# Second MLP of a decoder trunk: 11 of 16 pairs of up blocks by a 2x2 block scheme over tokens

## The chip, the cores and the metric

The program runs on one core of one Trainium2 chip. The metric is device time in microseconds (us), the median of three runs. The profile is one further execution of the same program, taken by the hardware profiler; its span runs from its first to its last instruction.

## The reference

Only the part that the change touches is given in full. The trunk has two layers; each has a mixer (multi-scale pooling in the first, stick-breaking attention in the second) and a squared-ReLU MLP, and each of the four is set between RMS norms.

```python
D_MODEL, SEQ, DEPTH = 1024, 512, 2
D_FF = 4 * D_MODEL
...
def sq_relu_mlp(h, w_up, w_down):
    u = jnp.matmul(h, w_up)
    return jnp.matmul(jnp.square(jax.nn.relu(u)), w_down)
...
        h = rms_norm(x, mlp_pre_g[layer])
        x = x + rms_norm(sq_relu_mlp(h, w_up[layer], w_down[layer]), mlp_post_g[layer])
```

All values are float32, h has 512 rows (tokens) of 1024, w_up is 1024 x 4096 and w_down 4096 x 1024.

## The kernel before

**Two parts for every operand.** A float32 operand is split into a high part (rounded to the matmul's format) and a low part, the rest. A product takes three matmuls: high by high, high by low, low by high. A split is a copy to the high part on ACT and a subtraction on DVE (`split`, L411 to L413; for weights `weight`, L140 to L155, whose lines L152 and L154 are the two steps and L142 the load).

**Up blocks.** The hidden dimension of 4096 is cut into 32 blocks of 128, numbered j. The loop `up_block` (L835) computes one block transposed: 128 hidden units by 512 tokens in one PSUM bank, over 8 slices of 128 of the contraction, three matmuls each, so 24 matmuls of 512 columns (lines L840, L841 and L842). Their moving operand are the normalised inputs `xnh` and `xnl`, which are high and low parts of [128, 8, 512]. `up` (L750) then has ACT do ReLU out of PSUM (L759) and the square (L760).

**Down products.** `Seven` (L630) computes the down projection for a group of blocks by a 2x2 block scheme with seven products in place of eight (halves of the tokens, of the group's blocks and of the output columns). The groups hold 2, 3, 3, 3 and 3 pairs of blocks (`GROUPS`, L25), so 28 of the 32 blocks; the last four go through `contract` (L554) with plain products. A product i of a group needs a combination of squares, `left(i)` (L669, L678; on POOL in the second MLP), and a combination of down weights, `right(i)` (L690, L697; on DVE), each split into parts by `split`. `make(i)` calls both, two products ahead, with two buffers each. Its matmuls are on L724: 18 of 512 columns for a group of three pairs, 12 for the first group. Each result is added to `y` by DVE out of PSUM (L736), or copied the first time (L731, L733).

**Order.** `mlp(l, mp, update)` (L738) is called for both layers. For each group g it loops over the seven products; behind each of the first six it issues one `up` block of the next group (in group 0 one more ahead of the loop), and the operands of the product after the next. In the last group those are the four blocks for `contract`. The order in which an engine gets its instructions in this part is not written by hand: a planner lays them out by their readiness and by the order in which the program issues them. Matrices stream from HBM by SP's queue; up weights go through two buffers `raw` into three buffers of parts (`w`) and a fourth (`wx`). PSUM has 8 banks of 512 columns; a group's products hold up to four at once, an up block one. The tiles `xt` hold the residual stream, `y` are four tiles of their own. The work behind the last down products is `Update` (L465): norm, gain, residual sum, store.

In the second MLP the first four blocks (j 0 to 3) are done in halves of 256 tokens ahead of group 0, while the last tokens of the input are still being normalised. Then group 0 runs beside the blocks 4 to 9, groups 1 to 3 beside six blocks each, and group 4 beside the last four.

## Time and profile before

| what | value |
|---|---|
| median of three runs | 887.29 us (887.13 to 887.39) |
| the profiled execution, its own time | 887.58 us |
| its span | 885.8 us |
| second MLP's first four up blocks | 561.0 to 584.9 us |
| its groups 0 to 4 | 584.9 to 861.5 us |
| `contract`, norm, residual sum and stores | 861.5 to 885.8 us |
| granted TensorE clock, mean | 0.998 |

The engines are PE (matmul), PEld (its weight loads, which lie beside the matmuls), DVE, ACT, POOL and SP. A row of the grouped view gives line, engine, operation, output<-input, shapes and count, then busy time in all and mean ns of one, then idle time ahead of them and what ended it. A row of the view by windows gives for a stretch of time its length, and busy time and instruction count of each engine. In the timeline a row is the start in us, the duration, and the instruction; the end of a matmul is modelled, so the step from one start to the next is its price.

### The profile page before, as it was taken

The page shows a single profiled execution, that of the slowest core. Times are in us where ns is not written, and L with a number is a line of the kernel's source. Part 1 is how long each engine was busy: PE and PEld are TensorE (multiplying, and loading weights), DVE is VectorE, ACT ScalarE, POOL GpSimd, SP SyncE. Part 2 cuts the span into 40 slices and gives each one's busy share as a digit, 9 for nine tenths or more (in the row PEclk, how much of TensorE's full clock was granted, in tenths as well). Part 3 has the DMA queues.
Part 4 walks back from the last instruction along what each step waited for, and adds up shares of the span by engine and source line. Part 5 has one row for each costly group of instructions (what it writes and reads, how often), then busy time and mean ns, then how long its engine had stood idle before and what let it go on. Part 6 is the DMA issues. An engine that isn't in the chain of part 4 may idle for free.

```text
span 885.8 us, 11988 instructions
## 1 busy us (share of the span) xinstructions
PE 875.6 (99%) x4628; PEld 765.3 (86%) x4628; DVE 693.7 (78%) x711; ACT 526.9 (59%) x878; POOL 85.2 (10%) x83
## 2 busy tenths in 40 slices
PE   9999999999999999999999999999999999999996
PEld 7998888888888888888888888998888888888885
DVE  5965898988979967656999985774897867977866
ACT  6758657667888736355888454465554454544631
POOL 2200000000000005000000001020310401303103
PEclk9999999999999999999999999999999999999999
DMA  7453557369697730875645655634324053142202
GB/s 287 162 203 124 187 203 274 132 215 344 249 344 260 274 130 1 321 296 204 212 152 165 209 184 166 231 134 146 116 98 163 24 176 110 48 154 84 64 8 95
DMA packets 47391, 153.86 MB, mean 174 GB/s; under 512 B 4656, under 2 KB 8714, under 8 KB 47334
## 3 DMA queue, kind: packets, MB, share of 16 engines
q1 hardware_dynamic: 47186, 153.09, 48.7%
q8 instruction: 36, 0.59, 0.3%
q14 instruction: 21, 0.17, 0.1%
q10 hardware_dynamic: 148, 0.02, 0.0%
HBM read 122.54 MB, written 30.54 MB: 173 GB/s over the span
## 4 chain that ended last, share of the span: by engine, by line
PE 93%; DVE 3%; DMA 2%; ACT 1%; issue 1%; POOL 0%; POOLq 0%; DVEq 0%; SPq 0%; ACTq 0%
PE ps L724 28%; PE ps L840 15%; PE ps L841 15%; PE ps L842 15%; PE ps L1124 3%; PE ps L453 2%; PE ps L455 2%; PE ps L454 2%; PE ps L1285 2%; PE ps L1200 2%; PE ps L979 2%; PE ps L955 1%; PE ps L1276 1%; DMA w<-kept 1%; ACT xn L416 1%
## 5 line engine op out<-in xcount | busy, mean ns | idle before, releaser
L724 PE MATMUL ps<-w,a 128*128 128x512 f32 x1176 | 265.3, 379 | 0.3
L840 PE MATMUL ps<-xnh,w 128*128 128x512 f32 (+1 forms) x704 | 253.6, 362 | 0.0
L841 PE MATMUL ps<-xnl,w 128*128 128x512 f32 (+1 forms) x704 | 253.3, 360 | 0.1
L842 PE MATMUL ps<-xnh,w 128*128 128x512 f32 (+1 forms) x704 | 253.2, 360 | 0.0
L724 PEld LDWEIGHTS ps<-w,a 128*128 128x128 f32 x1176 | 222.1, 189 | 32.5 <-ACT a L412 1.1
L842 PEld LDWEIGHTS ps<-xnh,w 128*128 128x128 f32 x704 | 133.4, 190 | 15.6
L841 PEld LDWEIGHTS ps<-xnl,w 128*128 128x128 f32 x704 | 133.4, 190 | 15.5 <-DVE xnl L413 0.3
L840 PEld LDWEIGHTS ps<-xnh,w 128*128 128x128 f32 x704 | 132.8, 190 | 16.2 <-ACT xnh L412 0.4
L152 ACT CAST w<-raw 128x1024 fp32r<-128x1024 f32 x56 | 58.6, 1046 | 85.4 <-PE ps L842 84.7
L736 DVE TENSOR_TENSOR y<-ps,y 128x512 f32<-128x512 f32 x124 | 83.9, 687 | 31.6 <-PE ps L724 31.4
L154 DVE TENSOR_TENSOR w<-raw,w 128x1024 fp32r<-128x1024 f32 x56 | 69.2, 1238 | 46.3 <-ACT w L152 46.3
L412 ACT CAST w<-e 128x1536 fp32r<-128x1536 f32 (+1 forms) x30 | 41.7, 1391 | 43.6 <-DVE e L697 33.7
L413 DVE TENSOR_TENSOR a<-r,a 128x768 fp32r<-128x768 f32 (+1 forms) x60 | 60.8, 1014 | 0.9 <-ACT a L412 0.9
L413 DVE TENSOR_TENSOR w<-e,w 128x1536 fp32r<-128x1536 f32 (+1 forms) x30 | 50.9, 1698 | 9.8 <-ACT w L412 9.6
L412 ACT CAST a<-r 128x768 fp32r<-128x768 f32 (+1 forms) x60 | 47.1, 785 | 16.7 <-POOL r L678 10.5
L1223 DVE TENSOR_TENSOR_SCAN e<-u,begin 128x1280 f32<-128x1280 f32 x16 | 44.9, 2808 | 13.4 <-ACT u L1214 13.3
L483 POOL TENSOR_TENSOR y<-y,grow 128x512 f32<-128x512 f32 x8 | 12.1, 1510 | 340.7 <-ACT xn L416 340.6
L413 DVE TENSOR_TENSOR w<-w,w 128x1536 fp32r<-128x1536 f32 (+1 forms) x20 | 34.6, 1729 | 11.2 <-ACT w L412 11.0
L412 ACT CAST w<-xn 128x1536 fp32r<-128x1536 f32 (+1 forms) x20 | 27.9, 1394 | 25.4 <-PE ps L724 25.4
L412 ACT CAST w<-w 128x1536 fp32r<-128x1536 f32 (+1 forms) x20 | 27.9, 1394 | 20.8 <-PE ps L724 18.9
L413 DVE TENSOR_TENSOR w<-xn,w 128x1536 fp32r<-128x1536 f32 (+1 forms) x20 | 33.0, 1650 | 8.0 <-ACT w L412 7.9
L759 ACT ACTIVATE r<-ps 128x512 f32<-128x512 f32 x56 | 33.1, 591 | 7.4 <-PE ps L842 7.4
(190 smaller groups left out, 1228.3 us busy)
## 6 DMA issues: line engine op xcount, KB each, us to landing
raw<-in_wup SPq DMA_DIRECT2D x64, 512.0 KB, 3.3
w<-kept SPq DMA_DIRECT2D x42, 512.0 KB, 5.9
w<-in_wdn SPq DMA_DIRECT2D x8, 1536.0 KB, 6.1
xn<-in_wdn SPq DMA_DIRECT2D x16, 768.0 KB, 4.9
kept<-wx SPq DMA_DIRECT2D x20, 512.0 KB, 3.0
kept<-apart SPq DMA_DIRECT2D x16, 512.0 KB, 3.4
through<-turn SPq DMA_DIRECT2D x7, 896.0 KB, 3.5
moved<-through SPq DMA_DIRECT2D x28, 224.0 KB, 3.8
```

What stands on the lines that cost most here:

```text
L152: nc.scalar.copy(hi, raw)
L154: nc.vector.tensor_tensor(out=lo, in0=raw, in1=hi.bitcast(F32), op=ALU.subtract)
L412: latest["act"] = nc.scalar.copy(hi, src)
L413: latest["dve"] = nc.vector.tensor_tensor(out=lo, in0=src, in1=hi.bitcast(F32), op=ALU.subtract)
L724: nc.tensor.matmul(bank, a[:, x, q, TS[t]], by_twos(w[:, z, q], NS[0]), start=start and q == 0 and k == 0, stop=q == self.n - 1 and k == 2 ...
L736: nc.vector.tensor_tensor(out=part, in0=bank, in1=part, op=ALU.add)
L759: nc.scalar.activation(split_up(r, 256), in_order(pu, 256), ACT.Relu)
L840: nc.tensor.matmul(pu[:, cols], wh[:, k, :], xh, start=k == 0, stop=False)
L841: nc.tensor.matmul(pu[:, cols], wh[:, k, :], xl, start=False, stop=False)
L842: nc.tensor.matmul(pu[:, cols], wl[:, k, :], xh, start=False, stop=k == KC - 1)
L1124: nc.tensor.matmul(bank, a[x][q], in_turn(w[q // 2][z][:, cols], 512), start=(i == 0 or not linked) and q == 0 and n == 0, stop=q == 3 and ...
L1223: nc.vector.tensor_tensor_scan(out=e[:, ::-1], data0=us[a][:, 1:][:, ::-1], data1=begin[:, ::-1], initial=0.0, op0=ALU.mult, op1=ALU.max,)
```

## The change

**Pairs.** Of the second MLP's up blocks, j 0 to 9 stay as they are (`PAIRED = 10`). The blocks 10 to 31 are taken as 11 pairs, q 0 to 10. A pair is a product of 2x2 blocks: two blocks of hidden units, two halves of the contraction, two halves of the tokens (256 each). It is done with seven products (`Pair.PRODUCTS`): each product is 4 slices x 3 matmuls of 256 columns, so a pair takes 84 matmuls of 256 columns where it took 48 of 512.

**Sums of the inputs.** Four combinations of quarters of the inputs, t1 to t4, are made once, during group 0, by `Sums`: ten additions and subtractions of 1024 columns on DVE, then four splits (ACT and DVE). Their parts lie in the buffer `wx`, in the tiles that `y` had, and t4 in a quarter of `xnh` and `xnl` themselves.

**Sums of the weights.** For each pair, S1 to S4 are made from the two raw weight blocks by four DVE operations of 512 columns (S3 in place of a21). Five splits follow: A (the whole first block, 1024 columns), B (S3 and a22, 1024 columns), S1, S2 and S4 (512 columns each). For S2 the low part is a subtraction on DVE, as before. For the other four (`BY_DMA`) ACT makes the high part and then writes its negative into the low part's place, and a DMA issued from POOL adds the raw values to it there.

**Results.** The seven products are added up partly in PSUM: those of a pair lie in two halves of one bank, and product 2 in a second bank. Each product is followed by one read of 256 columns: copies by ACT behind 1, 6 and 7, additions by DVE behind 2, 4 and 5, the ReLU by ACT behind 3. ReLU and square follow when a quarter or a half of the result is whole.

**Order.** `FIVE` writes where the products go: in groups 1 to 3 three pairs (a, b, c) of the next group are spread over seven cells, one behind each product of `Seven`; group 4 has two pairs, for the last four blocks. The operands of the next pair are prepared behind products of the one before; those of q 0 during group 0. A pair's raw weights use both `raw` buffers, and are loaded behind product 5 of the pair two before.

**The residual.** In the second MLP `y` now lies in the tiles of `xt`; `xt` is stored to HBM ahead of group 0 and loaded again near the end of group 4, into the tiles that `y` had.

```diff
+PAIRED = 10
+BY_DMA = "A B S1 S4".split()
...
-        for j in range(NJ):
+        for j in range(PAIRED if l else NJ):
             want(("up", l, j), wup[l, j])
...
+    class Sums:
...
+            self.homes = {1: (own[1], rest[1]), 2: rest[2:], 3: (own[0], rest[0]), 4: (high["12"], low["12"])}
...
+            self.steps = [
+                [(3, "h22", "h12", minus), (3, 3, "l22", plus), (3, 3, "l12", minus)],
+                [3, (1, "h12", "h11", minus)],
+                [(1, 1, "l12", plus), (1, 1, "l11", minus)],
+                [(2, "h22", 1, minus), (2, 2, "l22", plus), 1],
+                [(4, "h21", 2, minus), (4, 4, "l21", plus), 2],
+                [4],
+                [],
+            ]
...
+    class Pair:
...
+        PRODUCTS = {
+            1: ("a11", "b11", 0), 2: ("a12", "b21", 2), 3: ("s4", "b22", 0), 4: ("a22", "t4", 1),
+            5: ("s1", "t1", 0), 6: ("s2", "t2", 0), 7: ("s3", "t3", 1),
+        }
...
+        def load(self):
+            self.raw = [wts.tile([P, D], F32, tag="raw", bufs=2, name=name("raw")) for _ in range(2)]
+            for n, raw in enumerate(self.raw):
+                nc.sync.dma_start(raw, wup[self.l, self.j + n])
+
+        def split(self, what, src, hi, lo):
+            nc.scalar.copy(hi, src)
+            if what in BY_DMA:
+                nc.scalar.mul(lo, hi.bitcast(F32), -1.0)
+                nc.gpsimd.dma_start(lo, src, accum_op=ALU.add)
+            else:
+                nc.vector.tensor_tensor(out=lo, in0=src, in1=hi.bitcast(F32), op=ALU.subtract)
...
+        def prepare(self, behind):
+            on = nc.vector.tensor_tensor
+            if behind == 0:
+                self.load()
+                return
+            (a11, a12), (a21, a22) = ([x[:, c] for c in NS] for x in self.raw)
+            if behind == 1:
+                self.block(0)
+                both = spare_tile()
+                self.s1, self.s2 = both[:, NS[0]], both[:, NS[1]]
+                on(out=self.s1, in0=a21, in1=a22, op=ALU.add)
+                on(out=a21, in0=a11, in1=a21, op=ALU.subtract)
+            elif behind == 2:
+                self.block(1)
+                on(out=self.s2, in0=self.s1, in1=a11, op=ALU.subtract)
+            elif behind == 6:
+                self.third("S2", self.s2)
+            elif behind == 5:
+                self.third("S1", self.s1)
+                self.s4 = work.tile([P, D], F32, tag="grow", name=name("s4"))[:, NS[0]]
+                on(out=self.s4, in0=a12, in1=self.s2, op=ALU.subtract)
+            elif behind == 3:
+                self.third("S4", self.s4)
...
+        def product(self, i):
+            left, right, at = self.PRODUCTS[i]
+            if at == 2:
+                self.other = ps()
+            bank = self.other[:, :256] if at == 2 else self.bank[:, 256 * at : 256 * at + 256]
...
+            for k in range(4):
+                ws, xs = TS[k], [in_turn(x[:, k], 256) for x in (xh, xl)]
+                nc.tensor.matmul(bank, wh[:, ws], xs[0], start=start and k == 0, stop=False, skip_group_check=True)
+                nc.tensor.matmul(bank, wh[:, ws], xs[1], start=False, stop=False, skip_group_check=True)
+                nc.tensor.matmul(bank, wl[:, ws], xs[0], start=False, stop=k == 3, skip_group_check=True)
...
+            if i in (1, 6, 7):
+                nc.scalar.copy(out, src)
+            elif i in (2, 4, 5):
+                nc.vector.tensor_tensor(out=out, in0=src, in1=out, op=ALU.add)
...
+    FIVE = (
+        "a1 a2 a7 a6,a4 a5 b1 b2,a3 b7 b6,b4 b5 c1,c2 b3 c7,c6 c4 c5,c3",
+        "a1 a2 a7,a6 a4 a5,a3 b1 b2,b7 b6 b4 b5,b3,,",
+    )
     def mlp(l, mp, update):
...
-        y = y_tiles()
+        y = y_tiles() if l == 0 else [x[:, :D] for x in xt]
...
+            saved = dram.tile([T, P, D], F32, tag="saved", name="saved")
+            for t in range(T):
+                nc.sync.dma_start(saved[t], xt[t][:, :D])
+            sums = Sums()
+            pairs = [Pair(j, l, mp, sums) for j in range(PAIRED, NJ, 2)]
...
+            plan.update({(0, n): [(-1, int(x)) for x in w] for n, w in enumerate(("", "", "", "0", "12", "65", "3"))})
...
+        def ready(g, i):
+            if g == 0:
+                sums.step()
+            for q, which in plan[g, i]:
+                if q >= 0:
+                    multiply(g, q, which)
+                if which != 7 and which != 4 and q + 1 < len(pairs):
+                    pairs[q + 1].prepare(which)
+                if which == 5 and q + 2 < len(pairs):
+                    pairs[q + 2].prepare(0)
...
+                            for t in range(T):
+                                xt[t] = work.tile([P, D], F32, tag=f"y{t}", name=name("x"))
+                                nc.sync.dma_start(xt[t], saved[t])
...
-    nc = bacc.Bacc("TRN2", target_bir_lowering=False, num_devices=1, dynamic_dma_scratch_size=256)
+    nc = bacc.Bacc("TRN2", target_bir_lowering=False, num_devices=1, dynamic_dma_scratch_size=1024)
```

More of the change, by code (lines that the diff above doesn't have):

```diff
@@ L736, in product, with __init__, operand, step @@
                     nc.vector.tensor_tensor(out=part, in0=bank, in1=part, op=ALU.add)
+    class Sums:
+        def __init__(self):
+            quarter = lambda x: {
+                f"{k + 1}{n + 1}": x[:, 4 * k : 4 * k + 4, n * 256 : n * 256 + 256] for k in range(2) for n in range(2)
+            }
+            high, low = quarter(xnh), quarter(xnl)
+            whole = lambda x: x.rearrange("p (k c) -> p k c", k=4)
+            both = wts.tile([P, 2, D], F32R, tag="wx", name=name("sums"))
+            own = [whole(both[:, n]) for n in range(2)]
+            rest = [whole(work.tile([P, D], F32R, tag=f"y{n}", name=name("sums"))) for n in range(T)]
+            self.parts = {f"b{k}": (high[k], low[k]) for k in ("11", "21", "22")}
+            self.homes = {1: (own[1], rest[1]), 2: rest[2:], 3: (own[0], rest[0]), 4: (high["12"], low["12"])}
+            self.h, self.l = ({k: v.bitcast(F32) for k, v in x.items()} for x in (high, low))
+            self.raw, self.whole = {}, whole
+            plus, minus = ALU.add, ALU.subtract
+            self.steps = [
[7 more added lines that the diff above has]
+            ]
+        def operand(self, x):
+            if isinstance(x, str):
+                return (self.h if x[0] == "h" else self.l)[x[1:]]
+            if x not in self.raw:
+                self.raw[x] = self.whole(spare_tile() if x in (2, 3) else work.tile([P, D], F32, tag="grow", name=name("sum")))
+            return self.raw[x]
+        def step(self):
+            for x in self.steps.pop(0):
+                if isinstance(x, tuple):
+                    out, a, b = (self.operand(y) for y in x[:3])
+                    nc.vector.tensor_tensor(out=out, in0=a, in1=b, op=x[3])
+                else:
+                    hi, lo = self.homes[x]
+                    nc.scalar.copy(hi, self.raw[x])
+                    nc.vector.tensor_tensor(out=lo, in0=self.raw[x], in1=hi.bitcast(F32), op=ALU.subtract)
+                    self.parts[f"t{x}"] = hi, lo
@@ L748, in mlp, with square_parts @@
         written = {None}
+        def square_parts(j, r):
+            if not squares:
+                squares.extend([mp.tile([P, 3, 2, S], F32R, tag="r", bufs=2, name=name("sq")), *[None] * 4])
+            if j < plain + 3:
+                a = squares[0][:, j - plain]
+            else:
+                a = work.tile([P, 2, S], F32R, tag="spare", name=name("sq"))
+            split(r, a[:, 0], a[:, 1])
+            squares[1 + j - plain] = a[:, 0], a[:, 1]
         def up(j, pu=None):
@@ L787, in mlp, with multiply @@
         groups[0].load(1)
+        plan, pairs, sums = {}, [], None
+        if l == 1:
+            saved = dram.tile([T, P, D], F32, tag="saved", name="saved")
[3 more added lines that the diff above has]
+            pairs = [Pair(j, l, mp, sums) for j in range(PAIRED, NJ, 2)]
+            for g in range(1, len(GROUPS)):
+                for i, cell in enumerate(FIVE[g == len(GROUPS) - 1].split(",")):
+                    plan[g, i] = []
+                    for w in cell.split():
+                        q = 3 * (g - 1) + "abc".index(w[0])
+                        plan[g, i].append((q, int(w[1])))
+            plan.update({(0, n): [(-1, int(x)) for x in w] for n, w in enumerate(("", "", "", "0", "12", "65", "3"))})
[9 more added lines that the diff above has]
+                    pairs[q + 2].prepare(0)
+        def multiply(g, q, which):
+            pair = pairs[q]
+            if which == 1:
+                if pair.j < plain:
+                    part = groups[g + 1].part
+                    pair.begin([part(pair.j + n - firsts[g + 1]) for n in range(2)])
+                else:
+                    pair.begin([mp.tile([P, S], F32, tag="rp", bufs=2, name=name("rp")) for n in range(2)])
+            pair.product(which)
+            if pair.j >= plain and which in (5, 3):
+                n = which == 5
+                square_parts(pair.j + n, pair.r[n])
         early.clear()
@@ L806, in mlp @@
                         split_apart(mp)
+                if l == 1 and g > 0:
+                    ready(g, i)
+                    fill()
                 if i + 2 < 7:
@@ L809, in mlp @@
                         up(ups.pop(0))
+                    if l == 1 and g == 0:
+                        ready(g, i)
                     group.make(i + 2)
@@ L817, in mlp @@
                         up(ups.pop(0))
+                    if l == 1 and g == 0:
+                        ready(g, i)
                     if coming:
```

50 lines of the change are left out of this document (40 added, 10 removed).

## The prediction

> **What bounds the kernel now.** I read the page first, then the busy time of each engine by stage, then the timeline of the matmul engine, and last the groups by shape.
>
> ```profile
> span 885.8 us, 11988 instructions
> ...
> PE 93%; DVE 3%; DMA 2%; ACT 1%; issue 1%; POOL 0%; POOLq 0%; DVEq 0%; SPq 0%; ACTq 0%
> ```
>
> The second line is the chain that ended last: 93% of it is PE. The view by windows says the same of the stage that is changed, the second MLP's groups (length, then busy time of PE, PEld, DVE, ACT, POOL):
>
> ```profile
> 584.90:861.50 276.60, 276.46 (x1282) 241.75 (x1281) 205.69 (x185) 141.26 (x169) 48.57 (x20) 1.00 0.30 103
> ```
>
> PE is idle for 0.14 us of 276.60; DVE is busy for 74%, ACT for 51%. So a PE step saved is worth its whole time as long as DVE and ACT keep up, and nothing but PE steps can be gained here. The price of a step is the distance between starts, from the timeline:
>
> ```profile
> 575.09 0.28 PE L842 MATMUL ps<-xnh,w 128*128 128x256 f32 x1
> ...
> 578.44 0.28 PE L842 MATMUL ps<-xnh,w 128*128 128x256 f32 x1
> ...
> 590.10 2.75 PE L724 MATMUL ps<-w,a 128*128 128x512 f32 x12
> 592.69 0.38 PE L840 MATMUL ps<-xnh,w 128*128 128x512 f32 x1
> ```
>
> From 590.10 to 592.69 there are 12 matmuls of 512 columns: 215.8 ns each. From 575.09 to 578.44 there are 30 of 256 columns (ten rounds over three lines, each with its own weight load): 111.7 ns each. So half the columns cost 52% of the time, and this kernel itself shows it, with the very lines that do up blocks.
>
> **PE's part of the change.** A pair takes 48 x 0.2158 = 10.36 us now and 84 x 0.1117 = 9.38 us after: 0.976 us less, 10.73 us for 11 pairs. The stage becomes 265.9 us, a group of three pairs 7 x 18 x 0.2158 + 3 x 9.38 = 55.3 us where it was 58.3. The profiled execution's own time is 887.58 us (its span and 1.8 us around it); less 10.73 it is 876.85, and the median lies 0.29 under the profiled one: 876.6. That is the floor. The rest of the working asks what of it is lost.
>
> **DVE and ACT.** The prices, from the groups by shape of the second MLP:
>
> ```profile
> L154 DVE TENSOR_TENSOR w<-raw,w 128x1024 fp32r<-128x1024 f32 x24 | 29.3, 1221 | 27.6 <-ACT w L152 27.6
> L413 DVE TENSOR_TENSOR a<-r,a 128x768 fp32r<-128x768 f32 x24 | 28.5, 1189 | 0.0
> L152 ACT CAST w<-raw 128x1024 fp32r<-128x1024 f32 x23 | 24.1, 1048 | 56.0 <-PE ps L842 56.0
> ```
> ```profile
> L760 ACT ACTIVATE r<-r 128x512 f32<-128x512 f32 x23 | 14.5, 631 | 0.7
> L759 ACT ACTIVATE r<-ps 128x512 f32<-128x512 f32 x22 | 13.0, 591 | 0.0
> ```
> ```profile
> L413 DVE TENSOR_TENSOR a<-r,a 128x512 fp32r<-128x512 f32 x3 | 2.1, 687 | 0.0
> L412 ACT CAST a<-r 128x512 fp32r<-128x512 f32 x3 | 1.8, 613 | 0.0
> ```
> ```profile
> L577 DVE TENSOR_TENSOR y<-ps,y 128x256 f32<-128x256 f32 x2 | 0.8, 418 | 0.0
> ```
>
> DVE loses 22 low parts, 22 x 1.22 = 26.9 us. It gains the sums of the inputs, ten operations and four low parts of 1024 columns, 14 x 1.22 = 17.1 us, and for each pair four sums and the low part of S2 (5 x 0.69) and three additions out of PSUM (3 x 0.42), 4.69 us, 51.6 for 11. New: 205.7 - 26.9 + 17.1 + 51.6 = 247.5 us of 265.9, 93%.
>
> ACT loses 22 x (1.05 + 0.59 + 0.63) = 49.9 us. It gains four copies for the sums (4.2) and for each pair A and B with their negatives (4 x 1.05), S1 and S4 with theirs and S2 (5 x 0.61), two operations of 512 columns (1.26), and seven of 256 columns, of which the trace has none: between 0.30, half of a 512 row, and 0.63, the whole. I take 0.61 of a 512 row, DVE's ratio of 418 to 687, together 2.6. That is 11.1 a pair, 122 in all: 217.6 of 265.9, 82%.
>
> Whether PE stays full beside a DVE at 93% and an ACT at 82% can be read from the first MLP, where the same planner orders the work:
>
> ```profile
> 110.00:132.00 22.00, 22.00 (x104) 19.26 (x103) 22.00 (x22) 10.60 (x13) 0.00 (x0) 1.00 0.51 191
> ...
> 265.00:310.00 45.00, 45.00 (x210) 39.42 (x209) 42.73 (x42) 37.21 (x65) 0.00 (x0) 1.00 0.74 269
> ```
>
> It does: DVE at 100% in the one stretch, at 95% beside ACT at 83% in the other, and PE loses nothing. So the load as such costs nothing on average. One stage lies over it: group 0, where the sums are made.
>
> ```profile
> 584.90:639.10 54.20, 54.06 (x252) 46.99 (x251) 35.73 (x35) 32.20 (x46) 11.26 (x7) 1.00 0.42 146
> ...
> 697.20:755.50 58.30, 58.30 (x272) 51.05 (x271) 44.03 (x39) 28.59 (x32) 10.33 (x5) 1.00 0.31 109
> ```
>
> DVE there: 35.7 + 17.1 + 3.4 for the first pair's preparation = 56.2 of 54.2 us. Weights are prepared up to four blocks ahead, so at least three of the blocks from 10 on have their low parts made here now, and these go: 52.6. At the 95% of the row above that takes 55.3 us, 1.1 over. Ends 0 and 2.0; I take 1.1. In groups 1 to 3 DVE has 44.0 - 6 x 1.22 + 3 x 4.69 = 50.8 of 55.3 us, 92%: nothing lost.
>
> **The shared bank.** The products of a pair fill two halves of one PSUM bank, and each is read by ACT or DVE before the sum goes on. Counting through the order, 23 times a product directly follows another in the other half of the same bank (7 then 6, 6 then 4, 4 then 5: six times in each of groups 1 to 3, five in group 4). If only the columns that are read must be free, none of these waits; if the whole bank must be, all 23 do. The Trainium skill (PSUM — Partial Sum Buffer, PSUM bank collisions raise a hardware error) says that two engines may not use one bank at once, whatever the columns, and that semaphores must guard by bank; no run here shows it, and by that rule all 23 wait. A wait's price, from the chain of the last stage:
>
> ```profile
> 875.35 0.23 PE ps L455
> 875.58 0.02 issue
> 875.61 0.70 DVE y L577
> ```
>
> DVE starts 0.03 us after the last matmul's end; a matmul of 256 columns ends 0.28 - 0.11 = 0.17 us after the next could start; the read takes 0.42 (the 256-column row); with 0.03 back that is 0.65 us, 15.0 us for all 23. What speaks against paying it is that the planner may put other matmuls in the gap, as it does now:
>
> ```profile
> 639.93 0.59 PE L724 MATMUL ps<-w,a 128*128 128x512 f32 x2
> 640.36 0.38 PE L842 MATMUL ps<-xnh,w 128*128 128x512 f32 x1
> 640.58 0.59 PE L724 MATMUL ps<-w,a 128*128 128x512 f32 x2
> ```
>
> Here matmuls of a down product lie between those of an up block. Ends 0 and 15.0 us; with PE idle for 0.14 us in the whole stage today the value lies near the lower end, and I take 15% unfilled, 2.2 us.
>
> **The group's border.** The next group's second product needs sums of its squares from POOL. Before, from the end of the last up block to that product PE had
>
> ```profile
> 689.09 7.77 PE ps L724 x36
> ...
> 702.04 3.88 PE ps L724 x18
> ```
>
> 12.95 us of other work. After it has 3.88 + 1.34 + 3.88 + 4 x 1.34 = 14.5 us behind product 5 of the last pair, 1.5 more. The path gains one addition (0.42) and up to three issues on POOL ahead of its sums. An issue of a DMA on POOL is not in this trace; the nearest rows are an issue on SP and, above it, POOL's shorter sum of squares:
>
> ```profile
> 664.27 0.33 SPq L142 DMA_DIRECT2D raw<-in_wup  x1
> ```
> ```profile
> L678 POOL TENSOR_TENSOR s<-r 128x768 f32<-128x768 f32 x4 | 7.9, 1966 | 157.7 <-ACT r L760 157.7
> ```
>
> At 0.33 the path is 1.4 us longer and fits; at 1.97 each it is 6.3 longer and costs 4.8 at three borders, 14.5 us. I take 0, by the row that is an issue; the other end goes into the range.
>
> **The accumulating DMAs.** Not in the trace either. The nearest row is a load of the same size:
>
> ```profile
> raw<-in_wup SPq DMA_DIRECT2D x64, 512.0 KB, 3.3
> ```
>
> A and B are 512 KB too; reading both operands could double its 3.3 us. Their low parts are due about a pair's time after the raw weights, 55.3 / 3 = 18.4 us: nothing at either price. Storing and reloading the residual, eight transfers of 512 KB, lies beside a DMA share of 0.30 (the stage's row) and long before its use: nothing; uncovered, the four reloads cost 4 x 3.3 = 13.2 us.
>
> **Sum.** 887.58 - 10.73 + 1.1 + 2.2 = 880.15 profiled, 879.9 as a median, so 880 us.
>
> **Rivals.**
>
> First, DVE is blocked by POOL. POOL's sums of squares (10.33 us in the row of 697.20) run beside DVE's:
>
> ```profile
> L697 DVE TENSOR_TENSOR e<-xn,e 128x1536 f32<-128x1536 f32 x4 | 11.5, 2884 | 0.1
> ...
> L697 DVE TENSOR_TENSOR e<-xn,w 128x1536 f32<-128x1536 f32 x4 | 7.0, 1758 | 4.8 <-DMA xn<-in_wdn 4.6
> ```
> ```profile
> L413 DVE TENSOR_TENSOR a<-s,a 128x768 fp32r<-128x768 f32 x4 | 3.8, 952 | 0.0
> ```
>
> The same shapes take 2.88 and 1.76, and 1.19 (row above) and 0.95: 4 x 1.12 + 24 x 0.24 = 10.2 us of stretching, 2.6 a group, of 10.33 that could block. If with a denser DVE all of it does, a group has 50.8 + 7.7 = 58.5 us of DVE in 55.3: 3.2 us at three groups, 9.6. The Trainium skill (SBUF — State Buffer, Who interferes with whom) states such a rule: with two SBUF inputs a DVE instruction contends with GpSimd's reads, and the second waits for the first; the trace agrees where 1.76 becomes 2.88. From a third of it to all: 883 to 889.5, at half 885. For it: DVE has a third of today's slack. Against: 100% of DVE without loss above, though with an idle POOL. Chance 22%.
>
> Second, slower: the bank's waits stay unfilled, because at 92% of DVE the next product's operands aren't ready either when the planner would pull them in. All 23 at 0.65 us give 887.3 - 10.7 + 1.1 + 15.0 = 893 us, and more where an operation of up to 1.2 us is under way on the reading engine. It decides from 9.6 / 15.0 = 64% unfilled on. Chance 16%.
>
> Third, slower too: the two raw buffers. A pair's raw weights stay until B's DMA has read them. Issue 0.33, load 3.3, two sums 1.4 and B's two steps on ACT 2.1 make 7.1 us of the pair's 18.4; 11.3 are left for POOL's issue, the DMA and every queue. If that takes 14, ten pairs wait 2.7 us each: 880 + 27 = 907. It is slower than before from (889 - 880) / 10 + 11.3 = 12.2 us on. Against it: a plain transfer of that size takes 3.3. Chance 12%.
>
> **How the numbers follow.** The forecast, 876.5 to 883, has 50%. A measurement of this kernel tells about 0.2%, 1.8 us. The first rival is faster for 11 of its 22 points and within 0.2% (885.5 to 889.1) for 11; the others are slower, 28. So faster 61%, same 11%, slower 28%. The range begins at the floor and reaches to 894.5, the far end of the issues on POOL (880 + 14.5), which takes in the second rival's 893; the third and the second's dearer half are left out, 20%.
>
> **What the profile after would show.** Right: 924 matmuls of 256 columns in pairs at steps of 112 ns; in the stage DVE busy near 248 us and ACT near 218; PE idle for some 3 us, in short gaps behind products 7, 6 and 4 and in group 0. Wrong: PE idle over 10 us there. If its releasers are ACT and DVE reading the pairs' bank, the second rival holds; if `a` or `w` of the down products behind stretched DVE rows, the first; if the pairs' weight parts behind a DMA, the third.

## The result and the profile after

| what | before | after |
|---|---|---|
| median | 887.31 us (887.13 to 887.39) | 943.13 us (941.12 to 943.80) |
| ratio, 95% interval | | 1.0626 (1.0607 to 1.0644) |
| the profiled execution, its span | 887.58, 885.8 | 941.12, 939.3 |
| mean granted TensorE clock | 0.998 | 0.972 |

The medians are of four runs each. The change makes the kernel 55.8 us slower; 880 was forecast, with a range to 894.5. The page's span and its chain of work that ended last, after:

```profile
span 939.3 us, 13155 instructions
...
PE 74%; issue 7%; DVE 7%; DMA 7%; ACT 3%; POOL 2%; POOLq 0%; DVEq 0%; SPq 0%; ACTq 0%
```

PE's share of the chain fell from 93% to 74%; DVE, DMA and issue took most of the rest. The view by windows (columns: stretch, length, busy time of PE, PEld, DVE, ACT and POOL with counts, granted clock, DMA share, GB/s), first before, then after, from the first down product of the second MLP to the last, and behind it:

```profile
590.00:861.30 271.30, 271.16 (x1257) 237.14 (x1256) 202.92 (x181) 137.45 (x162) 46.42 (x19) 1.00 0.29 101
...
861.30:885.80 24.50, 16.95 (x91) 14.98 (x89) 17.04 (x31) 4.95 (x14) 8.78 (x9) 0.92 0.24 86
```
```profile
590.80:906.00 315.20, 278.06 (x1622) 251.40 (x1621) 231.38 (x255) 198.98 (x294) 85.42 (x64) 0.93 0.58 152
...
906.00:939.30 33.30, 24.35 (x120) 20.86 (x119) 17.81 (x33) 6.41 (x17) 8.81 (x9) 0.89 0.17 63
```

The first stretch should have become 271.3 - 10.7 = 260.6 us. It is 54.6 longer, although work has moved from it into the second, which has 29 matmuls more and is 8.8 us longer. So the two are best taken together. PE is idle for 37.1 + 9.0 = 46.1 us, where it was idle for 0.1 + 7.6 = 7.7 before: 38.4 us more. And it is busy for 278.06 + 24.35 = 302.4 us, where 271.16 + 16.95 - 10.73 = 277.4 would do: 25.0 us more, beside clocks of 0.93 and 0.89. On average no engine is full: DVE 73%, ACT 63% in the first stretch. So it isn't the amount of work alone; instructions wait for one another. For whom PE waits, from the groups by shape (the last column: idle time ahead of them and what ended it):

```profile
L727 PE MATMUL ps<-w,a 128*128 128x512 f32 x588 | 142.2, 390 | 8.6 <-ACT a L415 4.7 <-DVE x L739 2.1 <-DVE w L416 1.8
L865 PE MATMUL ps<-xnh,w 128*128 128x256 f32 x132 | 38.2, 292 | 5.4 <-ACT w L810 3.0 <-ACT r L873 1.2 <-ACT rp L873 1.2
...
L865 PE MATMUL ps<-sums,part 128*128 128x256 f32 x88 | 26.1, 302 | 12.9 <-DVE r L875 9.3 <-ACT r L873 2.7 <-DVE rp L875 0.6
...
L865 PE MATMUL ps<-xnh,part 128*128 128x256 f32 x44 | 14.3, 326 | 8.1 <-DVE r L875 6.1 <-DVE rp L875 2.0
```

L865 is the first matmul line of a pair's product; L873 and L875 are ACT's copies and DVE's additions that read a pair's bank. Most of the idle time ends with such a read. By the list in the prediction that is the second rival. But DVE and ACT themselves stand in line for something else, and their reads stand behind it, as the waits say (in total, times, longest):

```profile
SPq L807 <- DMA w<-raw: 131.1, 16, 19.7
```
```profile
ACT w L810 <- DMA raw<-in_wup: 24.4, 5, 5.8
...
DVE e L700 <- DMA xn<-in_wdn: 11.9, 4, 6.3
...
DVE spare L838 <- DMA raw<-in_wup: 8.4, 4, 3.3
...
DVE spare L838 <- DMA part<-spare: 7.7, 2, 6.1
...
DVE s L848 <- DMA part<-s: 4.8, 3, 2.8
```

SP's loads of raw weights (L807) wait 131 us for accumulating DMAs (w<-raw) that still read the buffer. The loads of down weights (xn) go through the same queue behind them, and DVE waits for those too. One such case in the timeline of POOL, of SP, of ACT and of DVE, and the DMAs of these ten us (KB each, us to landing):

```profile
691.76 0.86 POOL L813 DMA_DIRECT2D w<-raw  x1 [3.95 <-ACT r L878]
```
```profile
700.58 0.34 SPq L807 DMA_DIRECT2D raw<-in_wup  x1
```
```profile
700.78 1.04 ACT L810 CAST w<-raw 128x1024 fp32r<-128x1024 f32 x1 [5.32 <-DMA raw<-in_wup]
```
```profile
704.70 1.76 DVE L416 TENSOR_TENSOR w<-e,w 128x1536 fp32r<-128x1536 f32 x1 [6.17 <-ACT w L415]
```
```profile
w<-raw POOLq DMA_DIRECT2D x1, 512.0 KB, 8.8
part<-spare POOLq DMA_DIRECT2D x1, 256.0 KB, 8.5
```

POOL issues the DMA at 691.76; beside three other transfers it needs 8.8 us, and only then, at 700.58, is the next load issued. Meanwhile ACT stands 5.3 us at a copy of raw weights whose own load was late, and DVE 6.2 us behind ACT, with all later work of both in line.

How such a wait gets to PE is seen best at the longest gap, from the timelines of DVE, POOL and PE:

```profile
725.63 2.79 DVE L838 TENSOR_TENSOR spare<-raw 128x512 f32<-128x512 f32 x1 [6.08 <-DMA part<-spare]
728.46 2.17 DVE L839 TENSOR_TENSOR raw<-raw,raw 128x512 f32<-128x512 f32 x1
...
731.16 0.41 DVE L875 TENSOR_TENSOR r<-ps,r 128x256 f32<-128x256 f32 x1
```
```profile
725.79 2.08 POOL L681 TENSOR_TENSOR r<-r 128x768 f32<-128x768 f32 x1
```
```profile
731.62 0.58 PE L865 MATMUL ps<-sums,part 128*128 128x256 f32 x1 [5.85 <-DVE r L875]
```

DVE stands 6.08 us until a DMA has read the tile that its next sum is to fill. Only behind that sum and two more does it come to the read of PSUM (731.16) for which PE has waited 5.85 us. The gap has a second part, by the first rival's mechanism: beside POOL's sums two of DVE's take 2.79 and 2.17 us, where the same two took 0.68 and 0.69 shortly before (706.38 and 708.65), 3.6 us more.

Such a gap costs PE more than its own length. Around it (windows, as above):

```profile
725.70:731.60 5.90, 0.07 (x1) 0.00 (x0) 5.83 (x4) 0.94 (x1) 4.30 (x3) 0.89 0.25 44
731.60:736.00 4.40, 3.86 (x16) 3.57 (x17) 1.75 (x4) 3.00 (x6) 0.88 (x1) 0.50 0.31 53
736.00:740.00 4.00, 4.00 (x17) 3.64 (x16) 1.89 (x2) 3.68 (x7) 2.10 (x2) 0.50 1.03 234
740.00:745.00 5.00, 5.00 (x31) 4.62 (x31) 1.37 (x3) 2.64 (x6) 2.35 (x3) 0.94 0.82 201
```

Behind 5.8 us of idle time (5.90 less 0.07) the granted clock is 0.50 for 8.4 us, so by an estimate (half of 8.4) some 4 us more are lost.

### The profile page after: what moved, and what is told of

It reads as the page before. It is cut to its first block, busy times and chain, and to the rows that moved or that the text cites. A ratio compares the mean times of both kernels' runs of the same rounds, so it can differ in the third digit from the quotient of the medians.

```text
span 939.3 us, 13155 instructions
## 1 busy us (share of the span) xinstructions
PE 891.0 (95%) x5024; PEld 785.7 (84%) x5024; DVE 728.2 (78%) x791; ACT 590.5 (63%) x1014; POOL 122.0 (13%) x127
## 4 chain that ended last, share of the span: by engine, by line
PE 74%; issue 7%; DVE 7%; DMA 7%; ACT 3%; POOL 2%; POOLq 0%; DVEq 0%; SPq 0%; ACTq 0%
PE ps L727 22%; PE ps L1050 9%; PE ps L1051 9%; PE ps L1052 9%; PE ps L1334 3%; PE ps L456 2%; PE ps L458 2%; PE ps L865 2%; PE ps L457 2%; DMA raw<-in_wup 2%; PE ps L867 2%; PE ps L866 2%; PE ps L1495 2%; PE ps L1410 2%; PE ps L1189 1%
## 5 line engine op out<-in xcount | busy, mean ns | idle before, releaser
L727 PE MATMUL ps<-w,a 128*128 128x512 f32 x1176 | 275.1, 385 | 8.7 <-ACT a L415 4.7
L1050 PE MATMUL ps<-xnh,w 128*128 128x512 f32 (+1 forms) x528 | 186.9, 356 | 0.0
L1051 PE MATMUL ps<-xnl,w 128*128 128x512 f32 (+1 forms) x528 | 186.6, 354 | 0.1
L1052 PE MATMUL ps<-xnh,w 128*128 128x512 f32 (+1 forms) x528 | 186.6, 354 | 0.0
L1052 PEld LDWEIGHTS ps<-xnh,w 128*128 128x128 f32 x528 | 100.2, 190 | 11.0 <-DVE w L157 0.2
L1051 PEld LDWEIGHTS ps<-xnl,w 128*128 128x128 f32 x528 | 100.2, 190 | 10.8 <-DVE xnl L416 0.3
L1050 PEld LDWEIGHTS ps<-xnh,w 128*128 128x128 f32 x528 | 99.5, 190 | 11.4 <-ACT xnh L415 0.4
L739 DVE TENSOR_TENSOR x<-ps,x 128x512 f32<-128x512 f32 x62 | 41.6, 685 | 13.7 <-PE ps L727 13.6
L157 DVE TENSOR_TENSOR w<-raw,w 128x1024 fp32r<-128x1024 f32 x34 | 41.5, 1220 | 13.8 <-ACT w L155 13.8
L739 DVE TENSOR_TENSOR y<-ps,y 128x512 f32<-128x512 f32 x62 | 41.7, 685 | 10.5 <-PE ps L727 10.4
L810 ACT CAST w<-raw 128x1024 fp32r<-128x1024 f32 x22 | 23.0, 1045 | 35.9 <-DMA raw<-in_wup 24.4
L865 PE MATMUL ps<-xnh,w 128*128 128x256 f32 x132 | 38.2, 292 | 5.4 <-ACT w L810 3.0
L432 POOL TENSOR_TENSOR stat<-stat,mhalf 128x1 f32<-128x1 f32 x20 | 12.0, 599 | 218.1 <-DVE stat L423 216.8
```

The source lines that it names most:

```text
L157: nc.vector.tensor_tensor(out=lo, in0=raw, in1=hi.bitcast(F32), op=ALU.subtract)
L727: nc.tensor.matmul(bank, a[:, x, q, TS[t]], by_twos(w[:, z, q], NS[0]), start=start and q == 0 and k == 0, stop=q == self.n - 1 and k == 2 ...
L739: nc.vector.tensor_tensor(out=part, in0=bank, in1=part, op=ALU.add)
L865: nc.tensor.matmul(bank, wh[:, ws], xs[0], start=start and k == 0, stop=False, skip_group_check=True)
L1050: nc.tensor.matmul(pu[:, cols], wh[:, k, :], xh, start=k == 0, stop=False)
L1051: nc.tensor.matmul(pu[:, cols], wh[:, k, :], xl, start=False, stop=False)
```

## The experiments

Theories: **H**, buffers held by the accumulating DMAs make loads and sums late, and ACT and DVE stand in line. **B**, neighbouring products in one PSUM bank make PE wait for each read. **D**, DVE or ACT has too much work. All edits are to the changed kernel; the kernel before took 887.3 to 887.8 us beside them. The runs without the additions leave the low parts of A, B, S1 and S4 undone, and the one with plain copies puts the whole weights there; they measure time only.

**One suspected cause at a time.**

```diff
-                nc.gpsimd.dma_start(lo, src, accum_op=ALU.add)
```


> Leaves the accumulating DMAs out: the low parts of A, B, S1 and S4 stay the negative of the high parts, everything else is as in the changed kernel. Theory H (held buffers: the raw weights, the sums' tile and S4's tile stay occupied until a DMA has read them, so the next pair's load comes late and ACT and DVE stand in line at an instruction that waits for it): with no DMA to wait for, 880 to 892 us, PE idle under 8 us in the groups, clock near 1. Theory B (the shared bank: each product waits for the read of the other half, whatever the DMAs do): above 920 us, with the gaps still ahead of the pairs' products. Theory D (DVE and ACT have too much work): above 920 us, since both have the same work.

905.89 us (ratio 1.0207, 1.0177 to 1.0236): 37.2 less than the change, but above 892. The DMAs are the largest part and not all. What PE still waits for in this run is, for 10.7 us, the reads of the pairs' banks, and for 7.8 us the operands of down products.

```diff
-BY_DMA = "A B S1 S4".split()
+BY_DMA = []
```


> All five low parts of a pair by a subtraction on DVE, no accumulating DMA. DVE gains 2 x 1.22 + 2 x 0.69 = 3.8 us a pair, so a group of three pairs has 50.8 + 11.5 = 62.3 us of DVE in 55.3 of PE; ACT loses 3.3 us a pair. Theory H: bound by DVE, 7 us a group over, 900 to 915 us, still well under the changed kernel's 943. Theory B: 943 or more, since the gaps stay and DVE answers later. Theory D: more than 943.

920.17 us (1.0367, 1.0337 to 1.0398): 23 less, although DVE does more. That is H's direction, but short of the 900 to 915 that it promised.

```diff
-            bank = self.other[:, :256] if at == 2 else self.bank[:, 256 * at : 256 * at + 256]
+            bank = self.bank[:, :256] if at == 0 else self.other[:, 256 * (at - 1) : 256 * at]
```


> Products 7 and 4 go to the other half of product 2's bank, so 7 then 6, 6 then 4 and 4 then 5 lie in different banks, and only 2 then 7 still follow each other in one bank (four times where it was 23). All else is the same. Theory B: most of the gaps go, 885 to 905 us. Theory H: the gaps move to other instructions, 930 to 945 us.

Products 7 and 4 now lie in product 2's bank. 924.16 us (1.0412, 1.0382 to 1.0443): 19.0 less, between both theories. What is left stands above all at product 7 behind the read of product 2, the one neighbour that still shares its bank (21.0 us of PE's idle time), and DVE comes late there for a held tile:

```profile
DVE spare L838 <- DMA part<-spare: 16.0, 4, 5.0
```

The fourth run takes the pairs out and leaves the sums of the inputs (without t4's split) and the residual's store and reload:

```diff
-PAIRED = 10
+PAIRED = 32
...
-            for q, which in plan[g, i]:
+            for q, which in ():
...
```


> No pairs: all 32 up blocks as before, but the residual lies in the tiles of the changed kernel, is stored and reloaded, and the sums of the inputs are made in group 0 (t4 without its split, since the plain blocks need its place). Theories H and B: neither part costs anything by itself, 887 to 889 us. Theory D: group 0 has 35.7 + 16 us of DVE and more, 889 to 893 us.

889.31 us (1.0019, 1.0007 to 1.0030): the side parts cost 2.0 us, at the border between the 887 to 889 of H and B and the 889 to 893 of D. The rest belongs to the pairs.

**Both at once, and which DMA.** The first edit and the banks together:

> Both earlier edits in one: the accumulating DMAs are left out (the low parts of A, B, S1 and S4 stay the negative of the high parts, so the output is not the reference's), and products 7 and 4 write the other half of product 2's bank, so that of the neighbours only 2 and 7 share a bank. The edits by themselves gave 905.9 (no DMAs) and 924.2 (banks), against 943.1 with neither. If buffers held by the DMAs (H) and the shared bank (B) are two costs that add, 943.1 - 37.2 - 19.0 = 886.9, so 884 to 891. If the waits at the bank are only H seen from TensorE's side, nothing is left for the banks to save and it stays at 900 to 906. If DVE or ACT have too much work (D), also above 900, since the edits take no DVE operation away.

895.16 us (1.0084, 1.0055 to 1.0113), between the ranges. They are two costs, adding up but for 8 us. The low parts by DVE with the banks apart (it is four subtractions a pair more, the two and two in the brackets, not five):

> The other halves of the banks, and all low parts by DVE: no accumulating DMA, no negatives on ACT, five DVE subtractions a pair more of work on DVE in place of it (two of 128x1024, two of 128x512). The edits by themselves gave 924.2 (banks) and 920.2 (low parts by DVE). Two costs that add (H and B): 943.1 - 19.0 - 22.9 = 901.2, so 897 to 906. If DVE's own work is what is left in the 920.2 (D), the banks save little of it: 912 to 920.

908.52 us (1.0235, 1.0199 to 1.0271), between both. Here D has its place, in the view by windows of group 1:

```profile
637.20:697.40 60.20, 55.26 (x355) 51.44 (x356) 60.20 (x69) 33.63 (x51) 8.01 (x3) 0.94 0.29 97
```

DVE is busy for all of 60.20 us. So the low parts must be shared between DVE and DMAs, and it matters which DMAs hold what. The banks apart and `BY_DMA = "A B"`:

> The other halves of the banks; A and B still by accumulating DMAs, S1 and S4 by DVE, so that the tile of s1 and s2 and the tile of s4 are read by no DMA and only the two raw buffers are held by one. With the banks alone (924.2) DVE stood 16.0 us at the operation that waits for the DMA out of that tile. H in the form 'the sums' tile': 904 to 912. H in the form 'the raw buffers come late': 918 to 924, next to the banks alone.

906.99 us (1.0217, 1.0178 to 1.0257), 17.2 less than with all four by DMA: the two sums' tiles were dear. Next, in the changed kernel, the same DMA without the addition (`nc.gpsimd.dma_start(lo, src.bitcast(F32R))`):

> The changed kernel with one word altered: the POOL-queue DMAs copy the source instead of adding it to the negative (the low parts are then the whole weight, so the output is not the reference's). Same issues, same order, same waits, the same buffers held from the same moment; only the transfer is another kind. The accumulating ones take 5.3 us (512 KB) and 5.1 and 3.5 us (256 KB) from issue to landing in the changed kernel, the plain loads 3.6. If it is the length of the accumulating transfer that holds the buffers too long: 925 to 935. If it is the standing in line (the negative first, POOL's wait for it, the issue, then the transfer), whatever the transfer: 938 to 943.

927.49 us (1.0448, 1.0418 to 1.0479): 15.6 less, with every wait and issue in place. The transfer's kind is on the page, after and in this run:

```profile
w<-raw POOLq DMA_DIRECT2D x22, 512.0 KB, 5.3
```
```profile
w<-raw POOLq DMA_DIRECT2D x22, 512.0 KB, 3.2
```

5.3 us with the addition, 3.2 without (medians from issue to landing). So some 2 us a transfer make 15.6 of the 37.2 us; the other 21.6 stay with a plain copy and go only when there is no transfer.

These runs also say on which side the DMAs cost. PE itself waits for a DMA's result once in the changed kernel, for 1.5 us. ACT and DVE wait for raw weights and for tiles that a DMA still reads (L810, L838 and L848 in the list of waits above): 45.3 us in the changed kernel, 25.0 with plain copies, 9.4 without transfers, beside 943.13, 927.49 and 905.89 us.

**No shared neighbours.** From here, but for one run of the changed kernel itself, the banks are those of the third run and the order is 1 2 6 7 5 4 3, in which 1, 6, 5 and 3 use one bank and 2, 7 and 4 the other, in turn (product 4 now ends the second block's results):

```diff
-BY_DMA = "A B S1 S4".split()
+BY_DMA = "A B S4".split()
...
-        "a1 a2 a7 a6,a4 a5 b1 b2,a3 b7 b6,b4 b5 c1,c2 b3 c7,c6 c4 c5,c3",
-        "a1 a2 a7,a6 a4 a5,a3 b1 b2,b7 b6 b4 b5,b3,,",
+        "a1 a2 a6 a7,a5 a4 b1 b2,a3 b6 b7,b5 b4 c1,c2 b3 c6,c7 c5 c4,c3",
+        "a1 a2 a6,a7 a5 a4,a3 b1 b2,b6 b7 b5 b4,b3,,",
...
```


> A, B and S4 by accumulating DMAs, S1 and S2 by DVE (the tile that S1 and S2 share is then read by no DMA), products 7 and 4 in product 2's bank, and the products of a pair in the order 1 2 6 7 5 4 3, so that no two neighbours of a pair share a bank at all. With A and B by DMA, S1, S2 and S4 by DVE, and products 2 and 7 still neighbours, it was 907.0, and of TensorE's idle time there 3.4, 0.3, 3.7 and 1.7 us stood at the products that share a bank. B (the bank): these 9 us go, and with the clock that they cost 893 to 899. H (buffers held and loads late, the bank only where it shows): the waits move to the operands, 902 to 907.

920.40 us (1.0372, 1.0342 to 1.0402): both theories missed; it is 13 us slower than `"A B"` in the old order. Three attempts at the moment of things: preparing a pair one product later; its products earlier within the group as well; and later preparation in the changed kernel alone.

```diff
-                if which != 7 and which != 4 and q + 1 < len(pairs):
-                    pairs[q + 1].prepare(which)
+                behind = {2: 1, 6: 2, 7: 6, 5: 5, 3: 3}.get(which, 4) if q >= 0 else which
+                if behind != 4 and q + 1 < len(pairs):
+                    pairs[q + 1].prepare(behind)
```

> As the one before, and each pair's weights are prepared one product later: the ACT copy of A and the sums that read the raw weights behind product 2 and not behind product 1, B's behind 6, S2's behind 7. The loads of the raw weights are issued where they were. In the changed kernel ACT stood 24.4 us in all (5 times, 5.8 us at most) at the copy of A, waiting for the raw weights, with all its other work behind it. H in the form 'the raw weights land after ACT and DVE ask for them': 3 to 8 us faster than the run before (887 to 895). If the loads' time is not what ACT and DVE wait for there, or TensorE now waits for the operands: no faster, or slower by a few us.

918.62 us (1.0352, 1.0322 to 1.0382).

```diff
-        "a1 a2 a6 a7,a5 a4 b1 b2,a3 b6 b7,b5 b4 c1,c2 b3 c6,c7 c5 c4,c3",
+        "a1 a2 a6 a7,a5 a4 b1 b2,a3 b6 b7 b5,b4 c1 c2,b3 c6 c7 c5,c4 c3,",
```

> As the one before, and within a group's seven places the pairs' products stand earlier (four of them behind each of the first three down products, none behind the last), so that the squares of the third pair are ready sooner for the next group's sums on POOL. Without DMAs and with the banks apart (895.2) TensorE still stood 1.1 and 0.3 us at each border of groups, waiting for these sums. If that border is a cost of its own: 2 to 5 us less than the run before. If four products in a place crowd ACT and DVE (D): slower than the run before by 2 to 10.

918.89 us (1.0355, 1.0325 to 1.0385). The third has the first's edit with `{2: 1, 7: 2, 6: 6, 5: 5, 3: 3}`:

> The changed kernel with nothing altered but the moment: A's copy and sums behind product 2 in place of 1, B's behind 7 in place of 2, S2's and the rest as they were. H (raw weights late at ACT and DVE): 925 to 935. B (shared bank): stays at 940 to 945, since the banks are as in the changed kernel. If the DMAs' results are now too late for TensorE instead: above 945.

943.57 us (1.0633, 1.0603 to 1.0664). None of them moves the time by more than 2 us. H's two ranges were missed, and the last run is where B put it. A reading that fits: asking later does not help while the same buffer comes free no sooner. The raw loads of the last run wait for the DMAs as long as in the changed kernel, 132.7 us against 131.1. Then the DMAs one by one in the new order, `"A B"` and `"A"`:

> The order 1 2 6 7 5 4 3 with 7 and 4 in product 2's bank (no neighbours in one bank), A and B by accumulating DMAs, S1, S2 and S4 by DVE. Against 907.0 (same DMAs, order 1 2 7 6 4 5 3) and 920.4 (this order, S4 by DMA too). If S4's DMA holding the one tile of s4 made the 13 us: 897 to 906. If the order made them (sums and squares come at other moments): 917 to 922.

924.73 us (1.0415, 1.0380 to 1.0449). So S4's DMA was not the cause of the 13 us. With the same DMAs the new order, and the squares that come with it at another moment, are 17.7 us slower than the old one.

> As the one before, and B's low part by DVE too, so that only A goes by an accumulating DMA. The buffer of A's raw weight is needed until s4 is formed in any case; the other one is then free as soon as DVE has read it, and the next load can start. DVE gets 1.2 us a pair more. H (B's DMA holds the buffer that the next load waits for; DVE waited 14.4 us for the raw weights with A and B by DMA): 3 to 8 us faster than the run before. D (DVE is the bound: with everything by DVE it was busy 60.2 of 60.2 us in a group): 1 to 6 us slower than the run before.

894.92 us (1.0079, 1.0050 to 1.0108): 29.8 us less without B's DMA, far more than the 3 to 8 that H promised, though DVE does 1.2 us a pair more. SP's waits, first with A and B by DMA, then with A:

```profile
SPq L807 <- DMA w<-raw: 55.0, 12, 8.0
SPq L807 <- DVE s L848: 40.7, 10, 6.1
```
```profile
SPq L807 <- DVE s L848: 33.7, 9, 8.6
SPq L807 <- DVE w L815: 28.0, 9, 9.7
SPq L807 <- DMA w<-raw: 27.4, 3, 13.4
```

Twelve waits of the raw loads for the DMA became three. But in all these loads wait as long as before, 94.0 us against 96.3: now for DVE's subtraction in B's buffer (L815). What fell is the waiting of ACT and DVE for raw weights, from 12.1 and 10.7 us to 2.6 and 1.5. So the direction is H's, in the form that the prediction's third rival had. The size is not explained by it alone: ACT also lost B's negative (some 1.05 us a pair) and POOL an issue, and these were not taken apart.

**What is left without DMAs.** The additions left out, no neighbours shared; then in addition the squares' sums on DVE in place of POOL:

```diff
-            on = nc.gpsimd if self.l else nc.vector
+            on = nc.vector
```

> No accumulating DMA at all (low parts of A, B, S1 and S4 stay the negative of the high parts; the output is not the reference's) and no neighbours in one bank. Against 895.2 with 2 and 7 still neighbours, where TensorE stood 0.6 us three times between these. B alone: 891 to 894. If the order of products costs something by itself, above 897.

890.61 us (1.0036, 1.0023 to 1.0048): B alone, just below its range.

> As the one before, and the sums of squares that feed the down products (POOL's three operations of 128x768 a group, 2.1 to 2.8 us each) on DVE. In the run with 895.2 TensorE stood 1.1 and 0.3 us at each border of groups and 4.2 us at the first, behind these sums. If POOL's sums are the rest: 882 to 889. If it is DVE's and ACT's other work there: no change within 2 us, or slower.

883.15 us (0.9944, 0.9925 to 0.9964), 7.5 less. A group of three pairs with POOL's sums, and two without:

```profile
699.20:755.90 56.70, 55.58 (x380) 52.02 (x379) 49.70 (x57) 44.51 (x69) 9.04 (x4) 1.00 0.33 112
```
```profile
691.70:747.00 55.30, 55.30 (x379) 51.95 (x378) 50.60 (x63) 44.50 (x68) 0.00 (x0) 1.00 0.33 115
747.00:802.40 55.40, 55.40 (x380) 51.99 (x379) 49.76 (x61) 44.46 (x68) 0.00 (x0) 1.00 0.33 115
```

PE is full for 55.3 us, the forecast length to a tenth. So in these groups nothing but waits, and the slower clock behind them, is between the change and its floor.

**A version that computes everything.** The new order, A and S4 by DMA, the squares' sums on DVE, and S4's raw sums in turns in the two halves of their tile:

```diff
-                self.s4 = work.tile([P, D], F32, tag="grow", name=name("s4"))[:, NS[0]]
+                if self.j == PAIRED:
+                    self.sums.s4 = work.tile([P, D], F32, tag="grow", name=name("s4"))
+                self.s4 = self.sums.s4[:, NS[self.j // 2 % 2]]
```


> A version that computes everything: only A and S4 by accumulating DMAs, B, S1 and S2 by DVE; S4's raw sums take turns in the two halves of their tile, so that the next pair's doesn't wait for the DMA; the order 1 2 6 7 5 4 3 with no neighbours in one bank; the squares' sums on DVE in place of POOL. With A alone by DMA and the squares' sums on POOL it was 894.9, DVE busy 57.0 of 58.5 us in a group; the bound without any DMA or low part was 890.6, and 883.2 with the squares' sums on DVE. H (a held buffer is what makes a DMA dear, and POOL's sums lengthen DVE's operations): 883 to 888, at or below the kernel before. D (DVE has too much work once B, S1 and S2 are its own): 889 to 895. If S4's DMA is dear although its tile takes turns: above 897.

888.08 us against 887.59, ratio 1.0006 (0.9996 to 1.0016), at the upper edge of H: 55 us better than the change, and no faster than the kernel before. DVE's operations beside POOL's sums and without them, with A alone by DMA and then in this version:

```profile
L848 DVE TENSOR_TENSOR s<-raw,spare 128x512 f32<-128x512 f32 x10 | 10.5, 1049 | 0.0
```
```profile
L850 DVE TENSOR_TENSOR s<-raw,spare 128x512 f32<-128x512 f32 x10 | 6.8, 683 | 0.0
```

The same operation takes 683 ns in place of 1049. What remains (in the profiled execution, 891.56 us), first in all groups and by PE's waits, then around two short gaps (windows behind them, and the matmuls that end them in the timeline):

```profile
590.00:860.50 270.50, 261.43 (x1634) 240.59 (x1633) 248.75 (x298) 184.17 (x275) 19.45 (x22) 0.99 0.51 145
```
```profile
L727 PE MATMUL ps<-w,a 128*128 128x512 f32 x588 | 136.5, 381 | 3.9 <-ACT a L415 3.8
...
L867 PE MATMUL ps<-sums,part 128*128 128x256 f32 x88 | 24.9, 283 | 4.7 <-ACT r L875 3.3 <-ACT rp L875 1.4
```
```profile
761.80:765.00 3.20, 3.19 (x14) 3.08 (x15) 3.20 (x4) 2.17 (x4) 0.00 (x0) 0.56 0.31 123
...
704.90:708.00 3.10, 3.03 (x24) 2.83 (x24) 3.10 (x5) 1.84 (x5) 0.00 (x0) 1.00 0.29 78
```
```profile
761.81 0.38 PE L867 MATMUL ps<-sums,part 128*128 128x256 f32 x1 [1.83 <-ACT r L875]
```
```profile
704.91 0.38 PE L867 MATMUL ps<-sums,part 128*128 128x256 f32 x1 [1.48 <-ACT r L875]
```

PE is idle for 9.1 us of 270.50: 4.7 at a group's first product 6, which waits for ACT's copy of product 1, and 3.9 at down products, which wait for parts of the squares. The last run puts a down product ahead of that 6:

```diff
-        "a1 a2 a6 a7,a5 a4 b1 b2,a3 b6 b7,b5 b4 c1,c2 b3 c6,c7 c5 c4,c3",
+        "a1 a2,a6 a7 a5 a4,b1 b2 a3,b6 b7 b5 b4,c1 c2 b3,c6 c7 c5 c4,c3",
...
```


> As the version before (888.1 against 887.6), with the products of a group spread over its seven places as 1 2 of the first pair, then a down product, and only then its 6: in the run before TensorE stood 1.5, 1.8 and 1.4 us at the first pair's 6, which waits for ACT's copy out of product 1's bank, and that copy stood in ACT's line behind a split that waited for DVE. If these waits are what is left above the kernel before: 882 to 886, faster than before. If the wait only moves to another product (ACT and DVE have as much work in line as before, and places with four products crowd them): 886 to 890.

892.58 us (1.0064, 1.0050 to 1.0077): no gain, and slower than either range. From the groups by shape, in its profiled execution (890.27 us):

```profile
L867 PE MATMUL ps<-sums,part 128*128 128x256 f32 x88 | 24.4, 277 | 1.4 <-ACT r L875 0.9 <-ACT rp L875 0.5
...
L867 PE MATMUL ps<-xnh,part 128*128 128x256 f32 x44 | 12.2, 277 | 1.7 <-DVE r L877 1.7
```

The waits for these copies fell to 1.4 us, and product 3 now waits 1.7 us for DVE; in all PE is idle for 9.4 us, as much as before. So the waits moved. Why the median is 4.5 us longer is not seen in these two traces, since their executions lie the other way round (890.27 and 891.56). No version that computes everything beat the kernel before.

## Why the prediction was wrong, step by step

Taken away one after the other, the DMAs, the shared neighbours and POOL's sums gave 943.13, 905.89, 890.61 and 883.15 us: steps of 37.2, 15.3 and 7.5, and 3.2 left above 880. The sizes hang on that order (the banks first gave 19.0), and without the DMAs the low parts are not computed.

- **PE's price: right.** 55.3 us for a group of three pairs was forecast, and 55.3 and 55.4 were measured where nothing waits.
- **DVE and ACT as a load: right in kind, beside the point.** 247.5 and 217.6 us were forecast, 231.4 and 199.0 measured over a stretch that differs little. But "the load as such costs nothing" was read from two windows in which DVE and ACT wait for PE and for one another, and for no DMA; the pairs' work waits for DMAs, and what stands behind a waiting instruction waits too. With all low parts on DVE the load did cost: DVE was full for the 60.20 us of a group.
- **The accumulating DMAs: the step that failed.** "Nothing at either price", for 3.3 us or its double against 18.4 us until the low parts are due. Without the DMAs the kernel was 37.2 us faster, and in the new order 29.8 without B's alone. The low parts are not what is late (PE waited 1.5 us for one): the *source* is held, and ACT and DVE stand for it, 45.3 us against 9.4 without DMAs. The third rival had this mechanism for the raw buffers, at 12% and for 27 us, "against it: a plain transfer takes 3.3". The transfer took 5.3 us in the median and 8.8 beside others. That the held source makes all of the 37.2 us was not shown: the price hangs on the order of the products as well, POOL's issues were not taken apart from the transfers, and a kernel with more raw buffers was not run.
- **The shared bank: 2.2 us taken of 15.0.** Without DMAs, banks apart and the order that goes with them saved 905.89 - 890.61 = 15.3 us, the far end. PE was idle for 0.14 us before and this was read as a planner that fills every gap; it did not fill these. That the saving is so near to 15.0 is partly luck: the idle time at such reads was 10.7 us, and the estimate had no slower clock in it. The rule of the Trainium skill cited there (PSUM — Partial Sum Buffer, PSUM bank collisions raise a hardware error) pointed to the far end. What the runs show is that this program waits for the bank; whether the chip would need it was not tried.
- **The group's border and POOL: 0 taken.** An issue on POOL is 0.86 us, between the ends given. Moving POOL's sums to DVE was worth 7.5 us without DMAs, the border and the stretched operations of the first rival together; the two were not taken apart.
- **Group 0: 1.1 us taken.** From its first down product to group 1's, first after, then in the run without pairs:

```profile
590.80:646.10 55.30, 47.58 (x205) 39.30 (x203) 39.49 (x40) 32.88 (x48) 22.07 (x10) 0.93 0.49 146
```
```profile
590.10:637.20 47.10, 44.53 (x205) 38.37 (x204) 36.26 (x33) 27.32 (x39) 16.27 (x6) 1.00 0.57 199
```

The sums, with the residual's store beside them, leave 2.6 us of PE idle there (47.10 less 44.53), not 1.1, though DVE is at 77% and not full. With the first pair's preparation and t4's split the stretch is 8.2 us longer, and PE idle for 7.7.
- **The clock: not in the sum at all.** All rivals priced a wait at its length; beside 38.4 us more of idle time PE was busy for 25.0 us more, at a lower clock.

Open: why the new order with A and B by DMA is 17.7 us slower than the old one, with fewer shared neighbours. The loads' wait for DMAs does not say it: it is longer in the faster run (83.3 us against 62.3 from 590 to 910). The traces say where PE stands: in the new order 11.9 us at products 5 and 6 for ACT's copies, where it was 3.4, and 11.4 at product 7 for DVE's additions, where it was 5.8. Product 6 needs the copy of product 1, and in the new order one product lies between them in place of two, so that a late copy may show sooner; this was not tested. Nor was `"A"` run in the old order, so what B's DMA costs there is not known.

## What to carry to other kernels

Price a transfer by how long it holds its source as well as by when its result is due, and add the next load behind it. On engines that work in order, ask of every new wait what stands in line behind it; a free engine share says nothing about that. And ask whether a scheme that saves PE steps has the buffers to be fed: here the saving was there where nothing waited (55.3 us a group for 58.3), and every complete version tried lost as much in waits or more.

## What the runs showed of the hardware

- In the changed kernel the granted clock was 0.50 for 8.4 us after PE had been idle for 5.8 us. In the version that computes everything it was 0.56 over the next 3.2 us after 1.83 us of idle time (ahead of 761.81), and stayed at 1.00 after 1.48 (ahead of 704.91). The Trainium skill (TensorE: Matmul & The Clock Gate, Part 1) puts the fall to half speed behind an idle window of some 3.4 us that runs freely; the half speed agrees, but here a gap of about half that length was enough once.
- A DMA from POOL's queue that adds took 5.3 us for 512 KB (median of 22), a copying one on the same queue 3.2.
- DVE's subtraction of 128x512 was 683 ns with no sums on POOL and 1049 on average in a run that has them; one sum of that shape took 2.79 us beside them. The Trainium skill (SBUF — State Buffer, Who interferes with whom) says that the two share ports; the rows agree.
